# VectorE's order at the sub-layer ends of a two-layer trunk: chain, x update, split, low parts

## The chip, the cores and the metric

The kernel runs on one core of a Trainium2 chip. The metric is the time on the device of one execution, in microseconds (us). Before the change it is 2076.88 us, the median of three runs (2075.53 to 2077.28).

## The reference, cut to what matters

256 rows of 2048 numbers (fp32) go through two layers. A layer is a mixer and an MLP, each between two RMS norms and added to x:

```python
for layer in range(2):
    h = rms_norm(x, mix_pre_g[layer])
    m = pool_conformer_mixer(h, ...) if layer == 0 else short_conv_mixer(h, ...)
    x = x + rms_norm(m, mix_post_g[layer])
    h = rms_norm(x, ffn_pre_g[layer])
    a = relu(h @ w1[layer])                       # 2048 -> 8192
    x = x + rms_norm((a * a) @ w2[layer], ffn_post_g[layer])
# pool_conformer: h @ w_in (2048 -> 3072); pooling means over 2/4/8/16 rows, mixed by 4 groups;
#                 gated causal convolution of 31 taps, layer norm, silu; concatenation @ w_out
# short_conv:     h @ w_in (2048 -> 6144); B * conv3(C * u); @ w_out
```

So there are three places where one sub-layer ends and the next begins: end 1 (mixer of layer 0 to its MLP), end 2 (that MLP to the short convolution), end 3 (short convolution to the second MLP). At each, x must be updated with the norm over a whole row before the next matmul may read it.

## The kernel before

**Tiles.** The rows are two blocks of 128, t0 and t1. An output block is 128 rows by 512 columns in PSUM (pg), summed over k in steps of 128. Every fp32 product is three matmuls: with whi and wlo the high and low part of the weights, and xh and xl those of the transposed activations, whi x xh, wlo x xh and whi x xl (L224 to L226 in mms). A block with 8 k tiles has 24 matmuls, with 16 it has 48.

**Weights.** prep_to (L166) streams them in order, one tile of 128x1024 fp32 (512 KB, two k tiles) at a time: the SP queue loads raw (L170, four buffers), ScalarE rounds it to whi (L173), VectorE (in a front part GpSimd) subtracts to get wlo (L178). A raw buffer is free again once its wlo is made. whi and wlo have nine buffers each. ahead asks for the tiles of 4 or 8 steps ahead.

**An end.** The blocks of t0 are finished before those of t1, so that t1's last two blocks run on TensorE while t0's row is closed. At end 1 the last blocks are (0,0), (1,0), (0,1), (1,1) as (column block, row block). A block's result is first added to an earlier partial sum (L647 at end 1, L656 at end 2), then squared and summed on ScalarE (L591, L658) and multiplied with the gain (L592, L659). mix_close (L594) makes the square root on ScalarE (L601) and four tiny VectorE steps (L320 to L324). close_row (L343) updates x in four pieces of 512 columns (L355) and queues, per piece, norm_chunk: four transposes on TensorE (L276), xh on ScalarE in four pieces (L262), xl on VectorE in four pieces (L265). The next sub-layer's first block for t0 is mms_wide (L229): a first pass with whi over all k, xh and xl by turns (L240, L241), then a second pass with wlo (L248). Its low weight parts are so needed only in the second pass.

**What sets the order.** No order is written out. A scheduler places each instruction in its engine's queue by priority and the times it estimates; an engine then runs its queue strictly in that order, and an instruction that waits holds all behind it. urgent (L329) raises the priority by URGENT for the chain of an end. The low weight parts are ordinary work: wherever the scheduler sees VectorE free, one goes in.

**Other places that the change touches.** pool_sum (L448 on) multiplies PSUM sums with 1/count (L463) into an SBUF tile, which split_plain splits into ph and pl (L271, L272). The output projection's second half goes through its blocks as (2,0), (2,1), (3,0), (3,1), (0,0), (1,0), (0,1), (1,1) (L635); the layer norm of t0 and of t1 comes just before. The first sigmoid (L518) needs another function table on ScalarE than the square root before it.

## Time and profile before

| | |
|---|---|
| median of three runs | 2076.88 us |
| the profiled execution | 2074.67 us |
| its span | 2072.9 us |
| TensorE busy | 2041.4 us (98%) |
| VectorE busy | 1174.0 us (57%) |
| ScalarE busy | 1008.3 us (49%) |
| GpSimd busy | 153.5 us (7%), nearly all in the first 207 us |
| granted TensorE clock, mean | 0.995 |
| read from memory | 386.60 MB, 188 GB/s over the span |

In the rows PE is TensorE, PEld its weight load, DVE VectorE, ACT ScalarE, POOL GpSimd and SP the engine that issues the weight loads. A timeline row has the start, the duration (of all xN together), the engine, the line, what is written and read, the number of instructions and, in brackets, the idle time before it and what ended it. A row of waits has the waiting engine and line, the releaser, the sum in us, how many times, and the longest. In a row of windows each engine's busy time is followed by the number of its instructions. Matmuls overlap in the pipeline: one is recorded with 0.39 us, and the next starts 0.227 us after it. An engine that is busy half the time can still be full for ten microseconds at an end, so averages over the span say little here.

### The profile page before, as it was taken

What the parts mean: (1) busy time and instruction counts of PE and PEld (TensorE: products, weight loads), DVE (VectorE), ACT (ScalarE), POOL (GpSimd) and SP (SyncE); (2) the same over time, 40 slices, a digit from 0 to 9 for tenths busy, and PEclk for the clock granted to TensorE, in tenths of its full rate; (3) what the DMA queues carried; (4) which work ended last, traced back from release to release, by engine and by line L of the source; (5) the groups of instructions that cost most, each with busy time, mean ns of one, the idle gap of its engine ahead of it and who ended that gap; (6) DMA issues with size and microseconds to landing.
All of it is one profiled execution on the core that took longest, in us unless ns stands there. A gap on an engine that the chain in (4) does not pass through costs nothing.

```text
span 2072.9 us, 24556 instructions
## 1 busy us (share of the span) xinstructions
PE 2041.4 (98%) x9253; PEld 1687.7 (81%) x9253; DVE 1174.0 (57%) x1522; ACT 1008.3 (49%) x1296; POOL 153.5 (7%) x83
## 2 busy tenths in 40 slices
PE   8999999999999999999999999999999999999998
PEld 7888778888888888887888888888888888888886
DVE  3797764455455455547655645674555464554545
ACT  6454664444444354445544444464544444353443
POOL 5887000000000000000000000000000000000000
PEclk9999999999999999999999999999999999999999
DMA  7665546556565556556454665655555565565653
GB/s 261 198 208 180 176 148 219 175 180 210 171 203 181 184 194 198 186 170 213 161 197 165 201 197 177 202 189 193 183 193 193 170 212 187 171 208 189 201 172 114
DMA packets 203078, 390.30 MB, mean 188 GB/s; under 512 B 12368, under 2 KB 14512, under 8 KB 202960
## 3 DMA queue, kind: packets, MB, share of 16 engines
q1 hardware_dynamic: 202656, 388.55, 56.7%
q8 instruction: 72, 1.18, 0.2%
q14 instruction: 46, 0.38, 0.1%
q0 software_dynamic: 256, 0.18, 0.0%
q10 hardware_dynamic: 48, 0.02, 0.0%
HBM read 386.60 MB, written 2.10 MB: 188 GB/s over the span
## 4 chain that ended last, share of the span: by engine, by line
PE 85%; DVE 2%; DMA 1%; issue 1%; ACT 0%; DVEq 0%; ACTq 0%
PE pg L224 27%; PE pg L226 27%; PE pg L225 27%; PE pt L276 2%; DVE wlo L178 1%; DVE x L355 1%; PE pg L248 1%; PE pg L241 0%; DMA gp<-in_mix_post_g_dram 0%; PE pg L240 0%; DMA raw<-in_ab_w_out_dram 0%; ACT whi L173 0%; DVE xl L265 0%; DMA raw<-in_sc_w_in_dram 0%; DVE m L592 0%
## 5 line engine op out<-in xcount | busy, mean ns | idle before, releaser
L178 DVE TENSOR_TENSOR wlo<-raw,whi 128x1024 fp32r<-128x1024 f32 x660 | 807.5, 1227 | 580.4 <-ACT whi L173 547.9
L173 ACT CAST whi<-raw 128x1024 fp32r<-128x1024 f32 x722 | 760.2, 1054 | 575.2 <-PE pg L226 383.1
L226 PE MATMUL pg<-whi,xl 128*128 128x512 f32 x1520 | 596.0, 393 | 0.0
L224 PE MATMUL pg<-whi,xh 128*128 128x512 f32 x1520 | 590.9, 390 | 0.8 <-ACT t L518 0.7
L225 PE MATMUL pg<-wlo,xh 128*128 128x512 f32 x1520 | 591.3, 390 | 0.0
L225 PE MATMUL pg<-wlo,ah 128*128 128x512 f32 x1024 | 398.3, 389 | 0.0
L224 PE MATMUL pg<-whi,ah 128*128 128x512 f32 x1024 | 398.1, 389 | 0.0
L226 PE MATMUL pg<-whi,al 128*128 128x512 f32 x1024 | 397.6, 391 | 0.0
L225 PEld LDWEIGHTS pg<-wlo,xh 128*128 128x128 f32 x1520 | 285.4, 188 | 59.1
L224 PEld LDWEIGHTS pg<-whi,xh 128*128 128x128 f32 x1520 | 285.5, 188 | 58.5 <-ACT t L518 1.1
L226 PEld LDWEIGHTS pg<-whi,xl 128*128 128x128 f32 x1520 | 285.4, 188 | 56.9
L225 PEld LDWEIGHTS pg<-wlo,ah 128*128 128x128 f32 x1024 | 192.2, 188 | 40.1
L224 PEld LDWEIGHTS pg<-whi,ah 128*128 128x128 f32 x1024 | 192.3, 188 | 39.3
L226 PEld LDWEIGHTS pg<-whi,al 128*128 128x128 f32 x1024 | 192.3, 188 | 39.3
L178 POOL TENSOR_TENSOR wlo<-raw,whi 128x1024 fp32r<-128x1024 f32 x62 | 147.7, 2421 | 46.4 <-ACT whi L173 46.1
L680 ACT ACTIVATE t<-pg,rr 128x512 f32<-128x512 f32 x64 | 43.9, 686 | 194.0 <-PE pg L226 192.8
L711 DVE TENSOR_TENSOR m<-pg,m 128x512 f32<-128x512 f32 x96 | 65.9, 687 | 74.6 <-PE pg L226 74.6
L224 PE MATMUL pg<-whi,yh 128*128 128x512 f32 x256 | 100.2, 392 | 1.6 <-ACT yh L271 1.5
L225 PE MATMUL pg<-wlo,yh 128*128 128x512 f32 x256 | 99.7, 390 | 0.0
L226 PE MATMUL pg<-whi,yl 128*128 128x512 f32 x256 | 98.5, 390 | 0.2 <-DVE yl L272 0.2
L421 DVE SCALAR_TENSOR_TENSOR acc<-pp,par,acc 128x256 f32<-128x256 f32 x240 | 96.3, 480 | 0.1
L272 DVE TENSOR_TENSOR al<-pt,ah 128x512 fp32r<-128x512 f32 x64 | 44.0, 688 | 74.8 <-ACT ah L271 74.7
(130 smaller groups left out, 902.9 us busy)
## 6 DMA issues: line engine op xcount, KB each, us to landing
raw<-in_ffn_w_dram SPq DMA_DIRECT2D x512, 512.0 KB, 4.7
raw<-in_sc_w_in_dram SPq DMA_DIRECT2D x96, 512.0 KB, 4.9
raw<-in_ab_w_in_dram SPq DMA_DIRECT2D x48, 512.0 KB, 4.6
raw<-in_ab_w_out_dram SPq DMA_DIRECT2D x32, 512.0 KB, 3.9
raw<-in_sc_w_out_dram SPq DMA_DIRECT2D x32, 512.0 KB, 5.4
x<-in_x_dram SPq DMA_DIRECT2D x8, 256.0 KB, 7.2
gp<-in_mix_post_g_dram SPq DMA_DIRECT2D x8, 256.0 KB, 5.9
gp<-in_ffn_post_g_dram SPq DMA_DIRECT2D x8, 256.0 KB, 4.6
```

Source lines behind the costliest of these rows:

```text
L173: act.copy(hi, raw)
L178: (pool if on_pool else eng).tensor_tensor(lo[:, s], raw[:, s], hi.bitcast(F32)[:, s], ALU.subtract)
L224: pe.matmul(ps, lh, wh, start=start and k == 0, stop=False)
L225: pe.matmul(ps, lh, wl, start=False, stop=False)
L226: pe.matmul(ps, ll, wh, start=False, stop=stop and k == n - 1)
L248: pe.matmul(ps, lhs(k)[0], wt[c][1][:, j * CB : (j + 1) * CB], start=False, stop=k == n - 1)
L272: dve.tensor_tensor(lo, src, hi.bitcast(F32), ALU.subtract)
L276: pe.transpose(p[:, j * P : (j + 1) * P], src[:, j * P : (j + 1) * P], ident)
L355: dve.scalar_tensor_tensor(xs[t][:, cs], ms[t][:, cs], s, xs[t][:, cs], ALU.mult, ALU.add)
L421: dve.scalar_tensor_tensor(a, src, wcol, a, ALU.mult, ALU.add)
L680: act.activation(rl, ps, AF.Relu, scale=rr[t])
L711: dve.tensor_tensor(dst, ps, dst, ALU.add)
```

## The change

It gives VectorE another order at the three ends, by dependencies that bind the scheduler alone (hold, after): of the next sub-layer's weight tiles, the low parts of the second to fifth come after t0's second x update, those from the sixth on, and the first tile of the segment after, behind the last xl piece of t0's chunk 3, and the x update of t1's first 512 columns as well. The priority of urgent work goes from 150 to 1000. There are six raw buffers in place of four. The first two tiles of the segments after end 1 and end 2 have their hi and lo parts in the pool of the activations, not in that of the weights. In the output projection the partial sum is added in PSUM, with priority, and (3,0) comes before (2,1). In the pooling part the scaling stays in PSUM, its factors are loaded early in two pieces, and ph and pl are in another pool. A sigmoid of one column right after the row scales loads its table early.

```diff
+    RAW = 6
...
     def nm(s):
...
-    pool_lo = set()
-    for key in ("f1_0_0_0", "sC0", "f1_1_0_0"):
-        pool_lo |= set()
+    lows, guards = {}, {}
+    guests = set(seg["f1_0_0_0"][:2]) | set(seg["sC0"][:2])
+    def after(inst, first):
+        tc.add_manual_dep(
+            inst.ins, first.ins.name,
+            mybir.DependencyInfo(mybir.DependencyClass.NoSync, mybir.DependencyReason.SCHED_ONLY),
+            reason="row chain first")
+    def hold(ids, first):
+        for i in ids:
+            if i in lows:
+                after(lows[i], first)
+            else:
+                guards[i] = first
...
     def prep_to(i):
...
-            raw = wp.tile([P, 2 * CB], F32, tag="raw", name=nm("raw"), bufs=4)
+            raw = wp.tile([P, 2 * CB], F32, tag="raw", name=nm("raw"), bufs=RAW)
             nc.sync.dma_start(raw.rearrange("p (j n) -> p j n", j=nj), src)
-            hi = wp.tile([P, 2 * CB], F32R, tag="whi", name=nm("whi"))
-            lo = wp.tile([P, 2 * CB], F32R, tag="wlo", name=nm("wlo"))
+            home, tags = (ap_, ("ah", "al")) if nxt[0] in guests else (wp, ("whi", "wlo"))
+            hi = home.tile([P, 2 * CB], F32R, tag=tags[0], name=nm("whi"))
+            lo = home.tile([P, 2 * CB], F32R, tag=tags[1], name=nm("wlo"))
             act.copy(hi, raw)
-            i_, on_pool = nxt[0], nxt[0] in pool_lo
-            def low(raw=raw, hi=hi, lo=lo, on_pool=on_pool, eng=lo_eng[0](i_)):
-                for s in ((slice(0, CB), slice(CB, 2 * CB)) if on_pool else (slice(None),)):
-                    (pool if on_pool else eng).tensor_tensor(
-                        lo[:, s], raw[:, s], hi.bitcast(F32)[:, s], ALU.subtract)
-            low()
+            i_ = nxt[0]
+            low = lo_eng[0](i_).tensor_tensor(lo, raw, hi.bitcast(F32), ALU.subtract)
+            lows[i_] = low
+            if i_ in guards:
+                after(low, guards[i_])
...
-    URGENT = 150
+    URGENT = 1000
...
             pj = p[:, j * P : (j + 1) * P]
-            dve.scalar_tensor_tensor(
+            low = dve.scalar_tensor_tensor(
...
+        return low
...
         act.copy(hi, src)
...
     def norm_chunk(t, c, gkey, gbase):
...
-        split_cols(p, 4 * (c % 2), xT[t, c // 2], [pcol(gkey, gbase + 4 * c + j) for j in range(4)])
+        return split_cols(p, 4 * (c % 2), xT[t, c // 2],
+                          [pcol(gkey, gbase + 4 * c + j) for j in range(4)])
...
+    split_end = [None]
...
     def urgent(fn, *args):
         with tc.high_priority(URGENT):
-            fn(*args)
+            return fn(*args)
...
-    def close_row(t, s, nxt_gain, final=False):
+    def close_row(t, s, nxt_gain, final=False, nxt_ids=()):
...
-            dve.scalar_tensor_tensor(xs[t][:, cs], ms[t][:, cs], s, xs[t][:, cs], ALU.mult, ALU.add)
+            upd = dve.scalar_tensor_tensor(xs[t][:, cs], ms[t][:, cs], s, xs[t][:, cs],
+                                           ALU.mult, ALU.add)
+            if nxt_ids:
+                if t == 0 and c == 1:
+                    hold(nxt_ids[1:5], upd)
+                if t == NT - 1 and c == 0:
+                    after(upd, split_end[0])
...
-                later(2 + (c + 1) // 2, lambda c=c: urgent(norm_chunk, t, c, *nxt_gain))
+                def piece(c=c):
+                    end = urgent(norm_chunk, t, c, *nxt_gain)
+                    if t == 0 and c == 3:
+                        split_end[0] = end
+                        hold(nxt_ids[5:], end)
+                later(2 + (c + 1) // 2, piece)
...
         row_scale(t)
+    act.activation(small(), rr[NT - 1], AF.Sigmoid)
...
-            raw = wp.tile([P, 2 * CB], F32, tag="raw", name=nm("rw"), bufs=4)
+            raw = wp.tile([P, 2 * CB], F32, tag="raw", name=nm("rw"), bufs=RAW)
...
+        for h in range(2):
+            ic = mp.tile([P, 2 * T], F32, tag="gp", name=nm("ic"))
+            nc.sync.dma_start(ic, inv_cnt[2 * h * T : 2 * (h + 1) * T].partition_broadcast(P))
+            icnt[h] = ic
...
-        ic = t512((P, T))
-        nc.sync.dma_start(ic, inv_cnt[g * T : (g + 1) * T].partition_broadcast(P))
+        ic = icnt[g // 2][:, (g % 2) * T : (g % 2 + 1) * T]
...
-        pd = t512((P, 2, T))
-        dve.tensor_tensor(
-            pd, p.rearrange("p (c n) -> p c n", c=2),
-            ic.unsqueeze(1).to_broadcast([P, 2, T]), ALU.mult,
-        )
-        ph = tp.tile([P, 2, T], F32R, tag="ph", name=nm("ph"), bufs=2)
-        pl = tp.tile([P, 2, T], F32R, tag="pl", name=nm("pl"), bufs=2)
+        pd = p.rearrange("p (c n) -> p c n", c=2)
+        dve.tensor_tensor(pd, pd, ic.unsqueeze(1).to_broadcast([P, 2, T]), ALU.mult)
+        ph, pl = t512((P, 2, T), F32R), t512((P, 2, T), F32R)
         split_plain(pd, ph, pl)
...
-    def mix_close(t, parts, nxt_gain, final=False):
+    def mix_close(t, parts, nxt_gain, final=False, nxt_ids=()):
...
-        close_row(t, r, nxt_gain, final)
+        close_row(t, r, nxt_gain, final, nxt_ids)
...
-    for cb, t in ((2, 0), (2, 1), (3, 0), (3, 1), (0, 0), (1, 0), (0, 1), (1, 1)):
+    for cb, t in ((2, 0), (3, 0), (2, 1), (3, 1), (0, 0), (1, 0), (0, 1), (1, 1)):
...
-            dve.tensor_tensor(o, ps, o, ALU.add)
-            ps = o
+            urgent(dve.tensor_tensor, ps, ps, o, ALU.add)
         urgent(mix_evac, t, cb, ps, gps[cb], parts)
         if cb == 1:
-            urgent(mix_close, t, parts, ("ffn_pre", 0))
+            urgent(mix_close, t, parts, ("ffn_pre", 0), False,
+                   seg["f1_0_0_0"] + seg["f1_0_0_1"][:1])
     def last_evac(t, cb, ps, gp, parts):
...
                 if cb == NCB - 1:
-                    urgent(mix_close, t, parts, nxt_gain, final)
+                    urgent(mix_close, t, parts, nxt_gain, final,
+                           () if final else seg["sC0"] + seg["su0"][:1])
...
             if cb == NCB - 1:
-                urgent(mix_close, t, parts, ("ffn_pre", KT))
+                urgent(mix_close, t, parts, ("ffn_pre", KT), False,
+                       seg["f1_1_0_0"] + seg["f1_1_0_1"][:1])
```

What moves on VectorE (t0's x is x0, t1's is x1; wlo are low weight parts, sm the small columns of the norm's chain; the lines of the changed file are 14 to 30 higher: L178 is now L192, L265 L279, L355 L373, L656 L686). At end 2, from the chain's reciprocal to t0's x update, before:

```order
L320 RECIPROCAL sm_1482_7735<-sm_1481_7733 128x1
L178 TENSOR_TENSOR wlo_1471_7687<-raw_1469_7684,whi_1470_7686 128x1024
L322 TENSOR_SCALAR sm_1483_7737<-sm_1482_7735,sm_1480_7731 128x1
L178 TENSOR_TENSOR wlo_1474_7693<-raw_1472_7690,whi_1473_7692 128x1024
L323 TENSOR_SCALAR sm_1483_7737<-sm_1483_7737 128x1
L656 TENSOR_TENSOR pg_1488_7749<-pg_1488_7749,m_465_2530 128x512
L178 TENSOR_TENSOR wlo_1493_7794<-raw_1491_7791,whi_1492_7793 128x1024
L324 TENSOR_SCALAR sm_1482_7735<-sm_1482_7735,sm_1483_7737 128x1
L178 TENSOR_TENSOR wlo_1496_7800<-raw_1494_7797,whi_1495_7799 128x1024
L659 TENSOR_TENSOR m_465_2530<-pg_1488_7749,gp_1461_7666 128x512
L300 TENSOR_REDUCE sm_1509_7884<-parts_463_2528 128x1
L355 SCALAR_TENSOR_TENSOR x0_85<-m_464_2529,sm_1482_7735,x0_85 128x512 x4
```

and now, from the same place to the first xl:

```order
L630 TENSOR_SCALAR sm_1475_7725<-parts_457_2521,sm_1473_7721 128x1
L338 RECIPROCAL sm_1477_7729<-sm_1476_7727 128x1
L340 TENSOR_SCALAR sm_1478_7731<-sm_1477_7729,sm_1475_7725 128x1
L341 TENSOR_SCALAR sm_1478_7731<-sm_1478_7731 128x1
L342 TENSOR_SCALAR sm_1477_7729<-sm_1477_7729,sm_1478_7731 128x1
L373 SCALAR_TENSOR_TENSOR x0_85<-m_459_2523,sm_1477_7729,x0_85 128x512 x4
L192 TENSOR_TENSOR wlo_1463_7675<-raw_1461_7672,whi_1462_7674 128x1024
L192 TENSOR_TENSOR wlo_1466_7681<-raw_1464_7678,whi_1465_7680 128x1024
L192 TENSOR_TENSOR wlo_1469_7687<-raw_1467_7684,whi_1468_7686 128x1024
L192 TENSOR_TENSOR wlo_1488_7788<-raw_1486_7785,whi_1487_7787 128x1024
L686 TENSOR_TENSOR pg_1483_7743<-pg_1483_7743,m_460_2524 128x512
L279 SCALAR_TENSOR_TENSOR xl_1480_7736<-pt_1484_7768,par_96,xh_1479_7735 128x128 x4
```

Nothing stands between the chain's steps and the x update any more; four low parts and t1's add now follow it, and stand before the first xl.

At end 1, from the last step of the chain to the first xl, before:

```order
L324 TENSOR_SCALAR sm_426_2357<-sm_426_2357,sm_427_2359 128x1
L592 TENSOR_TENSOR m_361_2078<-opart_302_1810,gp_404_2263 128x512
L178 TENSOR_TENSOR wlo_440_2422<-raw_438_2419,whi_439_2421 128x1024
L300 TENSOR_REDUCE sm_453_2506<-parts_359_2076 128x1
L355 SCALAR_TENSOR_TENSOR x0_85<-m_360_2077,sm_426_2357,x0_85 128x512 x4
L178 TENSOR_TENSOR wlo_443_2428<-raw_441_2425,whi_442_2427 128x1024
L597 TENSOR_SCALAR sm_452_2505<-sm_453_2506 128x1
L647 TENSOR_TENSOR opart_302_1810<-pg_447_2437,opart_302_1810 128x512
L178 TENSOR_TENSOR wlo_446_2434<-raw_444_2431,whi_445_2433 128x1024
L178 TENSOR_TENSOR wlo_472_2538<-raw_470_2535,whi_471_2537 128x1024
L265 SCALAR_TENSOR_TENSOR xl_429_2364<-pt_433_2396,par_96,xh_428_2363 128x128 x4
```

and now:

```order
L342 TENSOR_SCALAR sm_421_2351<-sm_421_2351,sm_422_2353 128x1
L373 SCALAR_TENSOR_TENSOR x0_85<-m_355_2071,sm_421_2351,x0_85 128x512 x4
L192 TENSOR_TENSOR wlo_408_2299<-raw_406_2296,whi_407_2298 128x1024
L192 TENSOR_TENSOR wlo_411_2305<-raw_409_2302,whi_410_2304 128x1024
L192 TENSOR_TENSOR wlo_414_2311<-raw_412_2308,whi_413_2310 128x1024
L350 TENSOR_TENSOR pg_427_2365<-pg_427_2365,opart_297_1804 128x512
L192 TENSOR_TENSOR wlo_432_2410<-raw_430_2407,whi_431_2409 128x1024
L350 TENSOR_TENSOR pg_442_2431<-pg_442_2431,opart_297_1804 128x512
L279 SCALAR_TENSOR_TENSOR xl_424_2358<-pt_428_2390,par_96,xh_423_2357 128x128 x4
```

T1's product, a low part and a reduction no longer stand before the update; three low parts, t1's first add, one more low part and t1's second add do before xl. Some rows further on, at the last xl pieces of t0's chunk 3, it now reads:

```order
L279 SCALAR_TENSOR_TENSOR xl_426_2360<-pt_445_2482,par_96,xh_425_2359 128x128 x2
L373 SCALAR_TENSOR_TENSOR x1_86<-m_356_2072,sm_451_2507,x1_86 128x512 x2
L279 SCALAR_TENSOR_TENSOR xl_426_2360<-pt_445_2482,par_96,xh_425_2359 128x128
L373 SCALAR_TENSOR_TENSOR x1_86<-m_356_2072,sm_451_2507,x1_86 128x512
L279 SCALAR_TENSOR_TENSOR xl_426_2360<-pt_445_2482,par_96,xh_425_2359 128x128
L373 SCALAR_TENSOR_TENSOR x1_86<-m_356_2072,sm_451_2507,x1_86 128x512
```

The dependency holds only the update of t1's first column piece, the last row here; the other three stand between the pieces of chunk 3's xl. Before, all four stood ahead of chunk 2's and chunk 3's xl.

In the pooling part (acc is the convolution's sum, t in the first excerpt a scaled sum in SBUF, pt a sum in PSUM), before:

```order
L463 TENSOR_TENSOR t_268_1597<-pt_267_1588,t_266_1586 128x512
L421 SCALAR_TENSOR_TENSOR acc_206_1122<-pp_422,par_96,acc_206_1122 128x256
L421 SCALAR_TENSOR_TENSOR acc_207_1123<-pp_422,par_96,acc_207_1123 128x256
L421 SCALAR_TENSOR_TENSOR acc_206_1122<-pp_422,par_96,acc_206_1122 128x256
L272 TENSOR_TENSOR pl_270_1600<-t_268_1597,ph_269_1599 128x512
L421 SCALAR_TENSOR_TENSOR acc_207_1123<-pp_422,par_96,acc_207_1123 128x256
L421 SCALAR_TENSOR_TENSOR acc_206_1122<-pp_422,par_96,acc_206_1122 128x256
L463 TENSOR_TENSOR t_274_1634<-pt_273_1625,t_272_1623 128x512
L421 SCALAR_TENSOR_TENSOR acc_207_1123<-pp_422,par_96,acc_207_1123 128x256
L421 SCALAR_TENSOR_TENSOR acc_206_1122<-pp_422,par_96,acc_206_1122 128x256
L421 SCALAR_TENSOR_TENSOR acc_207_1123<-pp_422,par_96,acc_207_1123 128x256
L272 TENSOR_TENSOR pl_276_1637<-t_274_1634,ph_275_1636 128x512
```

and now:

```order
L497 TENSOR_TENSOR pt_265_1586<-pt_265_1586,ic_194_1076 128x512
L452 SCALAR_TENSOR_TENSOR acc_209_1128<-pp_424,par_96,acc_209_1128 128x256
L452 SCALAR_TENSOR_TENSOR acc_210_1129<-pp_424,par_96,acc_210_1129 128x256
L497 TENSOR_TENSOR pt_269_1620<-pt_269_1620,ic_194_1076 128x512
L452 SCALAR_TENSOR_TENSOR acc_209_1128<-pp_424,par_96,acc_209_1128 128x256
L287 TENSOR_TENSOR t_267_1597<-pt_265_1586,t_266_1596 128x512
L452 SCALAR_TENSOR_TENSOR acc_210_1129<-pp_424,par_96,acc_210_1129 128x256
L452 SCALAR_TENSOR_TENSOR acc_209_1128<-pp_424,par_96,acc_209_1128 128x256
L287 TENSOR_TENSOR t_271_1631<-pt_269_1620,t_270_1630 128x512
```

The two scalings come closer together, and the subtraction (L287, L272 before) reads pt in PSUM where it read t in SBUF; five convolution steps instead of eight stand between the first scaling and the last subtraction.

## The prediction

> **What bounds the kernel now.** I read the first row of the page, then TensorE's waits, then the windows in which it is not full. The first row and the waits:
>
> ```profile
> PE 2041.4 (98%) x9253; PEld 1687.7 (81%) x9253; DVE 1174.0 (57%) x1522; ACT 1008.3 (49%) x1296; POOL 153.5 (7%) x83
> ...
> PE pg L241 <- DVE xl L265: 5.8, 4, 2.7
> PE pt L101 <- DMA t<-in_mix_pre_g_dram: 4.6, 1, 4.6
> PE pg L240 <- ACT xh L262: 4.0, 2, 2.2
> PE pt L492 <- DVE pl L272: 2.5, 1, 2.5
> PE pg L224 <- ACT yh L271: 1.5, 1, 1.5
> ...
> PE pg L224 <- ACT t L518: 0.7, 1, 0.7
> PE pg L226 <- DVE yl L272: 0.2, 1, 0.2
> ```
>
> TensorE is busy 2041.4 of the 2072.9 us span, so 31.5 us is all that any reordering can win, apart from time at a lower clock. 4.6 us is the first DMA, and the tail after the last matmul takes about ten more; the diff leaves both alone. What it can touch is xl and xh (9.8 us, the starts of the next sub-layer), pl and yh (4.0 us, the pooling and the layer norm) and t (0.7 us). The windows say where (columns: us, PE busy, weight loads, DVE, ACT, POOL, granted clock, DMA share, GB/s):
>
> ```profile
> 164.00:170.00 6.00, 3.53 (x22) 3.01 (x21) 6.00 (x11) 3.47 (x5) 6.00 (x3) 1.00 0.67 224
> ...
> 220.00:225.00 5.00, 3.84 (x17) 2.66 (x15) 3.42 (x9) 4.83 (x8) 0.00 (x0) 1.00 0.11 43
> ...
> 255.00:260.00 5.00, 3.24 (x17) 2.10 (x15) 5.00 (x8) 3.17 (x6) 0.00 (x0) 0.98 0.90 271
> 260.00:265.00 5.00, 2.03 (x4) 1.33 (x5) 5.00 (x12) 4.97 (x17) 0.00 (x0) 0.50 0.81 246
> 265.00:270.00 5.00, 4.90 (x22) 3.58 (x21) 4.86 (x14) 2.82 (x11) 0.00 (x0) 0.84 0.61 215
> 270.00:275.00 5.00, 4.85 (x25) 4.05 (x26) 3.96 (x18) 3.54 (x13) 0.00 (x0) 1.00 0.00 0
> 975.00:980.00 5.00, 4.56 (x22) 3.47 (x20) 4.73 (x10) 2.88 (x5) 0.00 (x0) 1.00 0.89 321
> 980.00:985.00 5.00, 1.74 (x9) 0.98 (x9) 5.00 (x8) 4.37 (x12) 0.11 (x1) 0.84 0.71 209
> 985.00:990.00 5.00, 3.79 (x11) 3.12 (x12) 4.86 (x16) 2.62 (x9) 0.00 (x0) 0.50 0.87 305
> ...
> 1350.00:1355.00 5.00, 4.11 (x20) 3.15 (x19) 5.00 (x15) 4.65 (x14) 0.00 (x0) 1.00 0.91 284
> ```
>
> End 1 (mixer to FFN 0) is idle 1.76+2.97+0.10+0.15 = 5.0 us, and end 2 (FFN 0 to short conv) 0.44+3.26+1.21 = 4.9. VectorE is full in both, and the granted clock falls to 0.50. What that costs is at most busy time times missing clock, 0.50x2.03+0.16x4.90 = 1.8 us at end 1 and 0.16x1.74+0.50x3.79 = 2.2 at end 2; I take three quarters, 1.3 and 1.6, since recorded matmul times overlap. So the ends cost 6.3 and 6.5. End 3 (short conv to FFN 1) is idle 0.89 at full clock.
>
> Why VectorE is late at end 2, from the timelines of DVE, ACT and PE; the last three rows are the same chain at end 3:
>
> ```profile
> 968.71 0.70 DVE L656 TENSOR_TENSOR pg<-pg,m 128x512 f32<-128x512 f32 x1 [2.52 <-PE pg L226]
> 971.02 0.29 ACT L601 ACTIVATE sm<-parts,sm 128x1 f32<-128x1 f32 x1
> 972.30 0.16 DVE L320 RECIPROCAL sm<-sm 128x1 f32<-128x1 f32 x1
> 972.51 1.22 DVE L178 TENSOR_TENSOR wlo<-raw,whi 128x1024 fp32r<-128x1024 f32 x1
> 979.09 2.73 DVE L355 SCALAR_TENSOR_TENSOR x<-m,sm,x 128x512 f32<-128x512 f32 x4
> 985.80 1.38 DVE L265 SCALAR_TENSOR_TENSOR xl<-pt,par,xh 128x128 fp32r<-128x128 f32 x5
> ...
> 978.93 0.39 PE L225 MATMUL pg<-wlo,ah 128*128 128x512 f32 x1
> 979.16 0.39 PE L226 MATMUL pg<-whi,al 128*128 128x512 f32 x1
> 983.04 0.51 PE L240 MATMUL pg<-whi,xh 128*128 128x512 f32 x1 [1.76 <-ACT xh L262]
> 986.21 0.80 PE L241 MATMUL pg<-whi,xl 128*128 128x512 f32 x1 [2.66 <-DVE xl L265]
> ...
> 1337.22 0.15 DVE L320 RECIPROCAL sm<-sm 128x1 f32<-128x1 f32 x1
> 1338.15 1.23 DVE L178 TENSOR_TENSOR wlo<-raw,whi 128x1024 fp32r<-128x1024 f32 x1
> 1339.30 2.74 DVE L355 SCALAR_TENSOR_TENSOR x<-m,sm,x 128x512 f32<-128x512 f32 x4
> ```
>
> t0's last block ends at T0 = 968.6. The square root is there at 971.3, yet the x update starts at 979.09: five low parts of 1.22 us, t1's add and its product stand before and between the four tiny steps of the chain, which alone take 0.93 (end 3, 1337.22 to 1338.15). Matmuls start 0.227 us apart, so t1's two blocks (48) cover only up to T0+10.9, where transposes need an x that is just ready; three more low parts then stand before xl.
>
> **The change part by part.** All sums are against the profiled execution.
>
> *Ends: x update first.* At end 2 the root comes at 971.02 as now, since add, square and one cast stay ahead of it. After its 0.29 the reciprocal follows at once or, at the latest, where it is today, 972.30; then 0.93 of small steps with nothing between. So the x update starts between T0+3.7 and T0+4.6; I take T0+4.3, and it ends at T0+7.05, before t1's blocks do. The transposes then wait for nothing. What is late next is xl: behind the update stand four held low parts (4 x 1.2) and one add (0.7), and a piece of xl takes 1.38/5 = 0.28, so the first is done at T0+12.9. TensorE is through t1's blocks and the transposes at about T0+11.8 and waits 1.1. Later in the same pass chunk 2's xh stands on ACT behind three casts and two squares (0.15 wait), and chunk 3's xl pieces alternate on VectorE with t1's x updates (2.73/4 = 0.68 each): a piece every 0.96 where a pair of matmuls takes 0.45, so waits of about 1.0, 0.95 and 0.5. Together 3.7 in small pieces. None is near the 4.9 us over which the clock fell, so I take no half clock: 6.5-3.7 = **2.8 gained**, bounds 0.5 (a first gap that still halves the clock) and 5.
>
> *End 1*, from its own rows:
>
> ```profile
> 248.56 0.69 DVE L592 TENSOR_TENSOR m<-opart,gp 128x512 f32<-128x512 f32 x1 [1.78 <-DMA gp<-in_mix_post_g_dram]
> 256.65 2.73 DVE L355 SCALAR_TENSOR_TENSOR x<-m,sm,x 128x512 f32<-128x512 f32 x4
> 263.36 0.86 DVE L265 SCALAR_TENSOR_TENSOR xl<-pt,par,xh 128x128 fp32r<-128x128 f32 x3
> ```
>
> Here T0 is 246.1. A second cast (1.0) stands before the root, so the update runs from T0+5.2 to T0+8.0 (before: T0+10.6 to T0+13.3). The gain vector's DMA, which kept m to T0+2.5, is still under the root's time. Behind the update come four low parts and both of t1's adds (4.8+1.3): xl at about T0+14.4, TensorE free at T0+11.7, wait 2.7; then chunk 3's pieces between t1's updates again, 2.15. Of 6.3 remain 4.85: **1.5 gained**. If 2.7 us of idleness halves the clock, nothing is gained; if t1's second add is not late, 2.5.
>
> In the rows above the clock had fallen after 4.9 us of idleness in two pieces with one matmul between, and had not after 0.89. [...]
>
> *End 3* has one low part ahead of its update today (1338.15) and no idle window before chunk 2. Moving that part behind the update brings x 1.1 earlier, for nothing. But three of t1's four updates (2.05) now stand before chunk 3's xl: **1.1 lost**, bounds 0 and 2.
>
> *Pooling.* The sums are scaled in PSUM, so the subtraction for pl reads PSUM and one SBUF tile instead of two SBUF tiles:
>
> ```profile
> 159.88 0.67 DVE L463 TENSOR_TENSOR t<-pt,t 128x512 f32<-128x512 f32 x1
> 161.65 1.64 DVE L272 TENSOR_TENSOR pl<-t,ph 128x512 fp32r<-128x512 f32 x1
> 163.21 0.87 DVE L421 SCALAR_TENSOR_TENSOR acc<-pp,par,acc 128x256 f32<-128x256 f32 x2
> 165.77 2.66 DVE L272 TENSOR_TENSOR pl<-t,ph 128x512 fp32r<-128x512 f32 x1
> ```
>
> GpSimd is busy all through this stretch (the window from 164). The same size took 0.67 with a PSUM operand and 1.64 and 2.66 without. The order from 159.88 is now two scalings, two subtractions and five convolution steps (0.43): 4 x 0.65 + 5 x 0.4 = 4.6, so the last pl is done near 164.5. Today it is done at 168.4, at the end of TensorE's wait of 2.5, so that wait goes: **2.5 gained**. Were the subtractions as slow as now, it would be done 3.0 later, at 167.5, and 1.0 gained. [...]
>
> *Output projection.* (3,0) now runs before (2,1): 24 matmuls, 5.4 us, between the layer norm of t0 and the first use of t1's yh. That covers the 1.5 and the 0.2 of the waits: **1.7 gained**, bounds 0.5 and 1.7.
>
> *Sigmoid table* loaded ahead: **0.7 gained**, bounds 0 and 0.7.
>
> *Six raw buffers and the gains' early load.* In the long stages TensorE is already full, so deeper loading buys nothing there. At the start two weight tiles (1 MB) go ahead of the last x chunks. The rate in the first 40 us, one slice per us:
>
> ```profile
> GB/s 0 37 131 142 352 363 404 396 380 315 352 393 387 381 385 387 391 387 381 389 385 289 2 133 352 119 227 348 350 229 289 88 174 301 131 307 182 207 231 195
> ```
>
> At 390 those chunks come 2.7 us later; the squares on them stand on ACT before xh of chunk 2. I take **0.4 lost**, bounds 0 and 1.5. The two guest tiles and the in-place adds change no instruction's length.
>
> Sum: -2.8 - 1.5 + 1.1 - 2.5 - 1.7 - 0.7 + 0.4 = -7.7, so 2074.67 - 7.7 = 2067.0. The median of the runs shown is 2.2 above the profiled execution: **2069.2 us**.
>
> **Rivals.** *The waits are replaced.* VectorE does the same work in the same stretch; xl is as late as x was. For it: the held low parts and adds before xl, t1's updates before chunk 3. Against it: the update is 6 us earlier and only 5 stand behind it. Ends 1 and 2 then give 0, end 3 loses 2, and 4.9-0.4 remain from the rest: 2074.4.
>
> *Slower.* ACT takes its instructions in order, and casts that wait for a held-back raw stand before its squares, root and xh at all three ends. A raw is freed only by a low part, and those are held until the update; the next load then needs a landing time:
>
> ```profile
> raw<-in_sc_w_in_dram SPq DMA_DIRECT2D x13, 512.0 KB, 4.8
> ```
>
> That is the median. At T0+8.3 plus 4.8 the cast is just in time for xh of chunk 2 at T0+17. With 7 or 8 us it is 3 late at each end, and with the half clock 1.5 more: 4.5 a time, 13.5 in all against my -7.7: 2082.7. From 1.2 us per end it takes the change back to within 0.2%, from 2.6 the kernel is slower than before. Against it: six buffers load two tiles more before the end begins.
>
> *Full gain.* The ends' remaining 3.7 and 4.85 shrink by half, 4.3 less: 2064.9; with end 3 unharmed 2063.8. For it: each wait there is a piece or two of other work ahead of xl. Against it: that work stands in VectorE's queue as shown, whatever the times are.
>
> **Chances.** Forecast and its near neighbours 0.55, waits replaced 0.23, slower 0.12, full gain 0.10. A change within 0.2% (4.2 us) cannot be told from none. Faster by more means below 2072.7: the forecast case and the full gain, 0.65. Same: the replaced waits and a tenth of the slower case, 0.24. Slower: the rest, 0.11. Terms' bounds give 2062.5 to 2072.5 for the likeliest case; the range takes in the replaced waits: 2061.5 to 2077.5.
>
> **What would show it.** x update of t0 starting within 6 us of T0 at ends 1 and 2; no wait of the transposes for x; first xl waits of 2.7 and 1.1; clock 1.00 in the windows around them; no wait of TensorE for pl, yh or the sigmoid; a larger wait than 0.9 at end 3. I am wrong if the clock still halves, if ACT waits for raws ahead of xh, or if a wait turns up in the long stages.

## The result, and the profile after

The changed kernel takes 2060.02 us (median, 2059.55 to 2060.63), the kernel before 2076.89 (2075.53 to 2077.28): a ratio of 0.992, 95% interval 0.9903 to 0.9937, or 16.9 us less. The forecast was 2069.2, 7.7 less; the measured time lies below its range of 2061.5 to 2077.5.

The page's first row and TensorE's waits of the kernel after:

```profile
PE 2037.4 (99%) x9253; PEld 1685.5 (82%) x9253; DVE 1169.9 (57%) x1522; ACT 1006.9 (49%) x1297; POOL 153.7 (7%) x83
...
PE pt L102 <- DMA t<-in_mix_pre_g_dram: 4.6, 1, 4.6
PE pg L255 <- DVE xl L279: 3.7, 6, 1.4
PE pt L291 <- DMA x<-in_x_dram: 1.6, 2, 1.4
PE pg L254 <- ACT xh L276: 0.2, 1, 0.2
```

The waits for pl, yh and the sigmoid's t are gone, those for xl and xh have shrunk from 9.8 us to 3.9. TensorE is also busy 4.0 us less with the same 9253 matmuls, because none of them runs at half clock between the start and the tail (before, 6.83 us passed at half clock at each of ends 1 and 2). The windows, with the same columns as before:

```profile
220.00:225.00 5.00, 5.00 (x24) 4.12 (x23) 3.43 (x5) 4.85 (x8) 0.00 (x0) 1.00 0.00 0
...
250.00:255.00 5.00, 3.63 (x21) 2.76 (x20) 5.00 (x11) 3.77 (x12) 0.00 (x0) 1.00 0.93 306
255.00:260.00 5.00, 4.94 (x26) 3.78 (x25) 3.80 (x14) 5.00 (x13) 0.00 (x0) 1.00 0.64 218
260.00:265.00 5.00, 4.11 (x16) 2.47 (x15) 4.81 (x12) 3.02 (x11) 0.00 (x0) 1.00 0.00 0
...
975.00:980.00 5.00, 4.11 (x18) 2.60 (x16) 4.02 (x14) 5.00 (x17) 0.00 (x0) 1.00 0.31 107
980.00:985.00 5.00, 4.16 (x20) 2.89 (x19) 5.00 (x8) 1.13 (x4) 0.10 (x1) 1.00 0.11 9
...
1340.00:1345.00 5.00, 4.98 (x26) 4.03 (x26) 5.00 (x9) 0.38 (x3) 0.00 (x0) 1.00 0.22 48
```

End 1 is idle 1.37+0.06+0.89 = 2.3 us (before 5.0), end 2 0.89+0.84 = 1.7 (4.9), end 3 0.02 (0.9), all at full clock. VectorE's timeline shows the chain as it was meant, with the add of t0's last block, the x update and the first xl of ends 1 and 2:

```profile
240.58 0.70 DVE L350 TENSOR_TENSOR pg<-pg,opart 128x512 f32<-128x512 f32 x1 [2.98 <-PE pg L240]
...
245.12 2.74 DVE L373 SCALAR_TENSOR_TENSOR x<-m,sm,x 128x512 f32<-128x512 f32 x4
...
253.51 2.15 DVE L279 SCALAR_TENSOR_TENSOR xl<-pt,par,xh 128x128 fp32r<-128x128 f32 x8
...
959.22 0.70 DVE L686 TENSOR_TENSOR pg<-pg,m 128x512 f32<-128x512 f32 x1 [2.98 <-PE pg L240]
...
962.81 2.74 DVE L373 SCALAR_TENSOR_TENSOR x<-m,sm,x 128x512 f32<-128x512 f32 x4
...
970.61 1.11 DVE L279 SCALAR_TENSOR_TENSOR xl<-pt,par,xh 128x128 fp32r<-128x128 f32 x4
```

Both traces hold the same number of matmuls, so the start of the matmul that follows the first n tells where the time went. The differences are worked out from the two lists; where the order of two blocks differs they are good to about 0.4 us.

| up to | n | before, us | after, us | after - before | this stage | forecast |
|---|---|---|---|---|---|---|
| the first blocks | 100 | 28.3 | 28.9 | +0.6 | +0.6 | +0.4 |
| the first sigmoid | 250 | 62.5 | 62.2 | -0.4 | -1.0 | -0.7 |
| the pooling | 750 | 170.2 | 167.5 | -2.7 | -2.3 | -2.5 |
| the layer norm | 1025 | 226.8 | 221.3 | -5.5 | -2.8 | -1.7 |
| end 1 | 1400 | 314.8 | 305.3 | -9.5 | -4.0 | -1.5 |
| end 2 | 4525 | 1014.4 | 1000.4 | -14.0 | -4.5 | -2.8 |
| end 3 | 6100 | 1363.2 | 1348.1 | -15.2 | -1.1 | +1.1 |

So 15 us is what the profiled executions differ by (2074.67 and 2059.65). The other 1.9 of the 16.9 come from the kernel before: its profiled execution was 2.2 below its median, that of the change 0.4.

### The profile page after: what moved, and what is told of

Same layout as the page of the kernel before. It is cut to its first block, busy times and chain, and to the rows that moved or that the text cites. A ratio compares the mean times of both kernels' runs of the same rounds, so it can differ in the third digit from the quotient of the medians.

```text
span 2057.9 us, 24531 instructions
## 1 busy us (share of the span) xinstructions
PE 2037.4 (99%) x9253; PEld 1685.5 (82%) x9253; DVE 1169.9 (57%) x1522; ACT 1006.9 (49%) x1297; POOL 153.7 (7%) x83
## 4 chain that ended last, share of the span: by engine, by line
PE 98%; ACT 1%; DMA 1%; DVE 1%; SPq 0%; issue 0%; DVEq 0%; ACTq 0%
PE pg L239 31%; PE pg L240 31%; PE pg L238 31%; PE pt L291 2%; PE pg L262 1%; PE pg L404 0%; PE pg L405 0%; DMA x<-in_x_dram 0%; PE pg L403 0%; ACT whi L190 0%; ACT xh L276 0%; DVE x L373 0%; PE pg L255 0%; DMA raw<-in_sc_w_in_dram 0%; PE pt L522 0%; PE pt L493 0%
## 5 line engine op out<-in xcount | busy, mean ns | idle before, releaser
L192 DVE TENSOR_TENSOR wlo<-raw,whi 128x1024 fp32r<-128x1024 f32 x660 | 803.6, 1224 | 493.1 <-ACT whi L190 452.5
L192 POOL TENSOR_TENSOR wlo<-raw,whi 128x1024 fp32r<-128x1024 f32 x62 | 147.9, 2423 | 44.7 <-ACT whi L190 44.6
L286 ACT CAST ah<-pt 128x512 fp32r<-128x512 f32 x64 | 37.4, 584 | 135.2 <-PE pt L291 135.2
L287 DVE TENSOR_TENSOR al<-pt,ah 128x512 fp32r<-128x512 f32 x64 | 44.0, 687 | 96.5 <-ACT ah L286 96.4
```

The costliest lines, as they stand in the source:

```text
L192: low = lo_eng[0](i_).tensor_tensor(lo, raw, hi.bitcast(F32), ALU.subtract)
L286: act.copy(hi, src)
L287: dve.tensor_tensor(lo, src, hi.bitcast(F32), ALU.subtract)
```

## The experiments

Theory A: VectorE's held order carries the ends. Theory B: the buffers do, the six raws and the guest tiles. In each diff - stands for the kernel that it starts from. Those marked as one execution have one time and one profile beside the median of the kernel before; they are read by their traces.

**Without the dependencies.**

```diff
 # from the change
-                if t == 0 and c == 1:
-                    hold(nxt_ids[1:5], upd)
-                if t == NT - 1 and c == 0:
-                    after(upd, split_end[0])
+                pass
...
-                        hold(nxt_ids[5:], end)
```

> The change without its scheduling dependencies (no low part and no x update is held); all else stays. Theory A: the held order makes the gain at the three ends (4.0 + 4.4 + 1.1 = 9.5 us of the 15 by which the span fell). Then the x update of t0 starts late again, the clock halves again after ends 1 and 2, and the time is 2060.0 + 9.5 = 2069.5, between 2067 and 2071. Theory B: the six raw buffers, the guest tiles and the in-place adds carry the ends; then the time stays at or below 2062 and the clock stays full.

Measured: 2071.57 us (2071.17 to 2072.31), ratio to the kernel before 0.9974 (0.9964 to 0.9983). Against the trace of the change, end 1 costs 5.4 us more, end 2 5.0, end 3 1.8. TensorE's timeline, and one window:

```profile
254.78 1.97 PE L291 MATMUL pt<-ident,x 128*128 128x128 f32 x8 [3.77 <-DVE x L373]
258.94 0.79 PE L255 MATMUL pg<-whi,xl 128*128 128x512 f32 x1 [1.77 <-DVE xl L279]
...
981.36 0.79 PE L255 MATMUL pg<-whi,xl 128*128 128x512 f32 x1 [4.45 <-DVE xl L279]
...
255.00:260.00 5.00, 3.23 (x12) 2.53 (x12) 5.00 (x13) 4.07 (x16) 0.00 (x0) 0.50 0.88 306
```

The waits for x and xl are back, and the half clock with them. Without the dependencies the rest of the change makes the ends worse than they were. Theory A holds, with 11.5 in place of 9.5, which is a little above its range.

**The dependencies alone.** The functions hold and after, with their calls, in the kernel before; no other line of the change.

> The kernel before with the scheduling dependencies alone: four raw buffers, no guest tiles, the old priority, partial sums added in SBUF, old pooling, block order and sigmoid. Theory A: the ends gain nearly all of their 9.5 us, 2076.9 - 9.5 = 2067.4, between 2066 and 2069.5. Theory B: with four raw buffers the held low parts keep the raws, casts on ScalarE wait for loads ahead of xh and the ends gain less than half: 2072 or more.

Measured: 2066.11 us (2065.29 to 2067.48), ratio 0.9949 (0.9934 to 0.9963), 11.6 below the kernel before on that chip. By the trace ends 1 and 2 are as good as in the change (end 1 0.6 better), end 3 is not (1.4 worse). TensorE's waits:

```profile
PE pg L258 <- DVE xl L282: 3.4, 7, 0.7
PE pt L524 <- DVE pl L290: 2.5, 1, 2.5
PE pg L241 <- ACT yh L289: 1.5, 1, 1.5
```

Theory A holds. What is left to the whole change, 6.1 us by the times, is by the trace (8.1, its execution being the slowest of the four) 0.6 at the first sigmoid, 2.6 at the pooling, 4.1 at the layer norm and 1.4 at end 3.

**Four raw buffers.** One execution.

```diff
 # from the change
-    RAW = 6
+    RAW = 4
```

> The change with four raw buffers in place of six; VectorE's order at the ends is the same. Theory A: no effect beyond the start, where six cost about half a microsecond: 2059 to 2061. Theory B: the casts come late at the ends: 2063 or more, with waits of ScalarE for raws ahead of xh.

Measured: 2066.17 us, 6.1 more. Theory A was wrong here: the chains of the ends stand in the same order, but TensorE loses 5.1 us at the layer norm, 0.5 at end 2 and 1.3 at end 3. VectorE's timeline at the layer norm in this run and in the change, from the low part ahead of t0's steps to the reciprocal of t1's, with one wait of TensorE behind it in the run:

```profile
195.17 3.28 DVE L192 TENSOR_TENSOR wlo<-raw,whi 128x1024 fp32r<-128x1024 f32 x1 [4.32 <-ACT whi L190]
198.37 0.28 DVE L592 TENSOR_SCALAR t<-pt 128x128 f32<-128x128 f32 x1
...
210.24 0.95 DVE L596 RECIPROCAL t<-t 128x128 f32<-128x128 f32 x1
...
222.97 0.50 PE L238 MATMUL pg<-whi,yh 128*128 128x512 f32 x1 [2.10 <-ACT yh L286]
```

```profile
194.62 1.96 DVE L192 TENSOR_TENSOR wlo<-raw,whi 128x1024 fp32r<-128x1024 f32 x1 [4.91 <-ACT whi L190]
196.51 0.28 DVE L592 TENSOR_SCALAR t<-pt 128x128 f32<-128x128 f32 x1
...
207.97 0.95 DVE L596 RECIPROCAL t<-t 128x128 f32<-128x128 f32 x1 [0.31 <-ACT t L594]
```

The low part starts 0.5 later and takes 1.3 longer, so t0's steps start 1.9 later. In both runs GpSimd makes its own beside it (190.28 to 197.36 here, 190.78 to 198.8 in the change); the next one in the change, at 205.84 with GpSimd idle, took 1.23. With fewer buffers the scheduler also puts more casts and low parts between the steps, and t1's reciprocal is 2.3 later. TensorE waits 2.1 us for yh, with (3,0) before (2,1): the new block order does not cover that. ScalarE hardly waits for loads here (1.9 us from 185 to 240). So the buffers act through the order and a slow low part; which of the two weighs more was read from rows, not tried apart. At end 3 the load itself is late, on ScalarE ahead of the Square that VectorE's chain needs:

```profile
1339.30 1.05 ACT L190 CAST whi<-raw 128x1024 fp32r<-128x1024 f32 x1 [1.00 <-DMA raw<-in_ffn_w_dram]
```

**The old block order.** One execution.

```diff
 # from the change
-    for cb, t in ((2, 0), (3, 0), (2, 1), (3, 1), (0, 0), (1, 0), (0, 1), (1, 1)):
+    for cb, t in ((2, 0), (2, 1), (3, 0), (3, 1), (0, 0), (1, 0), (0, 1), (1, 1)):
```

> The change with the old block order of the output projection, (2,1) before (3,0). Theory A: the block between covers t1's yh, so TensorE waits for it again: 1.5 to 2.2 us more than the change, 2061.5 to 2062.5, with the wait behind the layer norm. Theory B: since with four raw buffers the wait for yh was there in spite of the new order (2.1 us), the six buffers are what removes it: 2060 within 0.7 and no such wait.

Measured: 2059.48 us, and by the trace no difference anywhere above 0.2 us. With six raw buffers the swap is worth nothing, which is theory B.

**Six raw buffers alone.** One execution. Six raw buffers do not fit beside the rest as it is (the pool of the work tiles needs 22 KB per partition, and 15.4 are left), so ph and pl share the buffers of the other 512-column tiles.

```diff
 # from the kernel before
-            raw = wp.tile([P, 2 * CB], F32, tag="raw", name=nm("raw"), bufs=4)
+            raw = wp.tile([P, 2 * CB], F32, tag="raw", name=nm("raw"), bufs=6)
...
-        ph = tp.tile([P, 2, T], F32R, tag="ph", name=nm("ph"), bufs=2)
-        pl = tp.tile([P, 2, T], F32R, tag="pl", name=nm("pl"), bufs=2)
+        ph, pl = t512((P, 2, T), F32R), t512((P, 2, T), F32R)
```

> The kernel before with six raw buffers and, for the space, ph and pl in the pool of the other 512-column tiles; nothing else. Theory A: the buffers alone take away the wait for yh behind the layer norm and the one at end 3, while VectorE's order at ends 1 and 2 leaves those as they were: 2.5 to 3.5 below the kernel before. Theory B, that of the prediction: the buffers gain nothing by themselves, within 0.8 of it.

Measured: 2074.13 us. That is 1.2 below the lowest of the six executions of the kernel before that ran beside it (2075.37 to 2078.81), but an execution of the kernel before on another chip took 2074.07; the span is only 0.5 below that of before. Its waits of TensorE:

```profile
PE pg L241 <- DVE xl L265: 9.6, 5, 4.4
...
PE pg L224 <- DVE m L591: 1.7, 1, 1.7
```

The wait for t1's yh has turned into one for m: a PSUM buffer of a finished block, which VectorE empties only behind the layer norm's steps. At ends 1 and 2 xl is waited for longer than before, 4.4 us each, and xh no longer. Neither theory fits well. The time says 2.8 less, the trace 0.5: by themselves the buffers move waits and gain little.

**Dependencies and six raw buffers.** One execution: the edits of the dependencies alone and of the six buffers alone, together on the kernel before.

> The kernel before with the scheduling dependencies and six raw buffers, ph and pl as in the run before; no guest tiles, old block order, old pooling arithmetic, no early sigmoid table. Theory A: these two parts carry the change: against it 2.5 to 3.5 for pooling and the table are missing and 3.6 for the guests are won, 2060 - 0.6, between 2058 and 2061.5. Theory B: the parts overlap, so that the buffers add less than 3 to the dependencies alone (2066.1): 2063 or more.

Measured: 2059.26 us, the time of the whole change. The two together gain 17.6 us, the dependencies alone 11.6: the buffers add 6.0 here, 6.8 by the two times themselves, against 0.5 to 2.8 alone. Theory A holds. Against the trace of the dependencies alone, 8.2 us longer, it gains 1.1 up to the first sigmoid, 1.8 at the pooling and the layer norm, 2.0 at end 1, 1.9 at end 2 and 1.5 at end 3.

**The pooling operand.** One execution.

```diff
 # from the change
-        pd = p.rearrange("p (c n) -> p c n", c=2)
-        dve.tensor_tensor(pd, pd, ic.unsqueeze(1).to_broadcast([P, 2, T]), ALU.mult)
+        pd = t512((P, 2, T))
+        dve.tensor_tensor(pd, p.rearrange("p (c n) -> p c n", c=2), ic.unsqueeze(1).to_broadcast([P, 2, T]), ALU.mult)
```

> The change with the scaled pooling sums written to an SBUF tile again, so that the subtraction for pl reads two SBUF operands beside GpSimd; all else stays. Theory A: pl takes 1.6 to 2.7 us instead of 0.7 and TensorE waits for it 0.5 to 2.5: 2060.5 to 2062.5. Theory B: the closer order of the scalings is the gain, pl is in time even when slow: 2060 within 0.7, no wait.

Measured: 2060.22 us. VectorE's timeline of the last two subtractions, and TensorE's wait for them; then the same two in the change:

```profile
159.76 2.62 DVE L287 TENSOR_TENSOR t<-t,t 128x512 fp32r<-128x512 f32 x1
164.08 1.12 DVE L287 TENSOR_TENSOR t<-t,t 128x512 fp32r<-128x512 f32 x1
...
PE pt L522 <- DVE t L287: 0.2, 1, 0.2
```

```profile
160.89 0.68 DVE L287 TENSOR_TENSOR t<-pt,t 128x512 fp32r<-128x512 f32 x1
162.27 0.68 DVE L287 TENSOR_TENSOR t<-pt,t 128x512 fp32r<-128x512 f32 x1
```

With two SBUF operands the subtraction is slow again beside GpSimd (busy from 152.83 to 171.76 in the change), 2.62 and 1.12 us in place of 0.68. The one for yl, of the same size and with two SBUF operands as well, takes 0.69 at 206.93 in this run, by when GpSimd has long finished in the change (198.8). The slow ones cost 0.2 of a wait, no more: the last pl is done at 165.2, and TensorE needs it at about 165. The gain at the pooling is from when these instructions run, not from their operand.

**The sigmoid's table.** One execution.

```diff
 # from the change
-    act.activation(small(), rr[NT - 1], AF.Sigmoid)
```

> The change without the early load of the sigmoid's table. Theory A: TensorE waits for the first sigmoid again, 0.7 to 1.0 more: 2060.7 to 2061. Theory B: other work covers it now, no such wait, 2060 within 0.5.

Measured: 2060.28 us; TensorE does not wait for the sigmoid, and until end 2 begins the trace shows no difference above 0.2 us. At end 2 this execution loses 0.7: two casts wait 0.39 and 0.69 us for their loads there, ahead of chunk 2's xh, and the clock falls to half (see the last section). The 1.0 that the change gains at the first sigmoid comes with six raw buffers as well: alone they have it too (the 250th matmul 1.2 us earlier relative to the 25th), and the row of that wait is missing from their list. With six buffers the early table load (1.28 us on ScalarE in the change) does nothing. With four raw buffers and the early load the wait is gone too, so there the load may do it; that was not tried apart.

**All of t1's updates held.** One execution, for the small waits left at the ends.

```diff
 # from the change
-                if t == NT - 1 and c == 0:
+                if t == NT - 1:
                     after(upd, split_end[0])
```

> The change with all four of t1's x updates held behind the last xl piece of t0, not the first alone. Theory A: the waits of 0.65 and 0.19 between those pieces at ends 1 and 2 go, 2060.0 - 1.7 = 2058.3, between 2057.5 and 2059. Theory B: they only move to t1's transposes, 2060 within 0.7.

Measured: 2059.44 us. The last pieces of xl are no longer waited for, but now low parts are. TensorE's waits:

```profile
PE pg L255 <- DVE xl L279: 2.0, 2, 1.4
...
PE pg L239 <- DVE wlo L192: 1.2, 3, 0.4
```

At ends 1 and 2 the trace gets 1.4 us ahead of the change for a moment and keeps 0.4 and 0.5 of it; end 3 gives 0.8 back. Theory B has the time right, but the waits moved to the low parts and not to t1's transposes: VectorE has then four updates (2.7 us) between the splits and the low parts of the second pass.

**Without guest tiles.** One execution first, then four.

```diff
 # from the change
-    guests = set(seg["f1_0_0_0"][:2]) | set(seg["sC0"][:2])
+    guests = set()
```

> The change without the guest tiles: the first two tiles of the segments after ends 1 and 2 have their hi and lo in the weight pool again. Without them t1's x updates come later in VectorE's order at ends 1 and 2. Theory A: the guests carry nothing, 2058.5 to 2061. Theory B: without them the whi of the last tiles come late, 2063 or more.

Measured: 2055.71 us. Both theories had it wrong: it is faster.

> The change without the guest tiles, timed in rounds. Theory A: the 4 us of the one look hold, 2055.5 to 2057, 1.0% below the kernel before, since low parts come before t1's updates and the first xl before t1's add. Theory B: they were chance, 2059 to 2060.5.

Measured: 2055.26 us (2054.31 to 2055.95), ratio 0.9895 (0.9877 to 0.9913). End 1 of that run, on VectorE:

```profile
251.80 1.12 DVE L279 SCALAR_TENSOR_TENSOR xl<-pt,par,xh 128x128 fp32r<-128x128 f32 x4
252.84 0.69 DVE L350 TENSOR_TENSOR pg<-pg,opart 128x512 f32<-128x512 f32 x1
...
258.91 3.48 DVE L192 TENSOR_TENSOR wlo<-raw,whi 128x1024 fp32r<-128x1024 f32 x3
...
263.63 2.73 DVE L373 SCALAR_TENSOR_TENSOR x<-m,sm,x 128x512 f32<-128x512 f32 x4
```

With no other edit the scheduler places t1's second add behind the first four xl pieces, and four low parts before t1's x updates. TensorE waits for no xl. That the guests cost the change nearly 5 us is shown; that they do it through this order is how the rows read, and was not tried apart.

**Three parts alone.** The dependencies, the six raw buffers and the pooling part on the kernel before: the change less guest tiles, block order, in-place and urgent adds, sigmoid, and with the old priority.

> Three parts of the change alone on the kernel before: the scheduling dependencies, six raw buffers, and the pooling part (scaling in PSUM, factors loaded early). Old block order, partial sums added in SBUF, old priority, no guest tiles, no early sigmoid table. Theory A: these three are all that pays; the wait for m behind the layer norm (1.7 with two of them) is gone, since the pooling part puts that m earlier into VectorE's order; the time is that of the change without guests, 2055.3, plus up to 0.7 for the table: 2055 to 2056.3. Theory B: the block order or the in-place adds are needed for the layer norm or end 1: 2057 or more.

Measured: 2055.08 us (2054.80 to 2055.93), ratio 0.9898 (0.9881 to 0.9914), 21.3 below the kernel before on that chip. All of TensorE's waits, and the m that TensorE waited 1.7 us for with the dependencies and six buffers alone:

```profile
PE pt L102 <- DMA t<-in_mix_pre_g_dram: 4.5, 1, 4.5
PE pt L291 <- DMA x<-in_x_dram: 1.1, 1, 1.1
PE pt L291 <- DVE x L373: 0.9, 2, 0.5
...
216.79 0.68 DVE L621 TENSOR_TENSOR m<-pg,gp 128x512 f32<-128x512 f32 x1
```

Theory A holds: three parts are all that pays. They beat the kernel before by 21 us and the whole change by 4 to 5. The in-place adds and the priority were left out only here, together with the rest, and not tried apart.

## Why the prediction was wrong

The direction, the places and most mechanisms were right; the size was not, and two causes were put down to the wrong part. By the prediction's own steps:

**What bounds the kernel.** Right. All gains are gaps of TensorE at the places named and the half clock behind them, and the long stages did not move.

**End 2 (2.8 forecast, 4.5 measured).** The price of the end, 6.5, was about right: 4.5 gained and 1.7 left make 6.2. The chain ran as worked out; with T0 = 959.1 the update starts at T0+3.7, the early end of the interval. The mis-sized term is the waits that stay, 3.7 forecast and 1.7 measured. The update came 0.6 before the T0+4.3 that was taken, and four low parts and an add took 5.1 us with their overlap (965.47 to 970.61) where 4 x 1.2 + 0.7 = 5.5 was taken, so the first piece of xl was done at T0+11.8 and not T0+12.9. TensorE is there at T0+11.9: a wait of 1.1 was forecast, none came.

```profile
971.02 0.48 PE L255 MATMUL pg<-whi,xl 128*128 128x512 f32 x1
```

Chunk 2 cost 0.17 for xh, as forecast, and 0.67 for its xl, which the sum did not have. Chunk 3's pieces, forecast at 2.45, cost 0.65 and 0.19. I had an update of t1 ahead of each piece, but two pieces are done before the first update stands in their way.

**End 1 (1.5 forecast, 4.0 measured).** The price of 6.3 was right (4.0 gained, 2.3 left), and again the update came earlier and the work behind it took less than was taken. With T0 = 240.5 the update started at T0+4.6 (5.2 forecast), and the first piece of xl was done at T0+13.3 (14.4). TensorE's waits in the change:

```profile
253.91 0.50 PE L255 MATMUL pg<-whi,xl 128*128 128x512 f32 x1 [1.36 <-DVE xl L279]
262.86 0.49 PE L255 MATMUL pg<-whi,xl 128*128 128x512 f32 x1 [0.65 <-DVE xl L279]
263.78 0.50 PE L255 MATMUL pg<-whi,xl 128*128 128x512 f32 x1 [0.19 <-DVE xl L279]
```

1.36 where 2.7 was forecast, 0.84 where 2.15 was: 2.2 in place of 4.85.

**The clock.** It stayed full, as the sum had it, but the premise was wrong and the step held by the smaller waits. I took the clock to have fallen over 4.9 us of idleness. In the trace of the kernel before it falls at 983.4, after waits of 0.44 and 1.76 and before the one of 2.66 begins. No run shows that the 2.7 us forecast for end 1 would leave the clock full: the longest wait after the first loads that did is 2.47 (pl in the kernel before), and behind 2.10 with four raw buffers and 2.46 with the dependencies alone it was halved.

**End 3 (1.1 lost forecast, 1.1 gained measured).** The step "three of t1's four updates now stand before chunk 3's xl" describes the order rightly, and the updates are where it says. They hold nothing up, since xl of chunk 2 now comes before t1's updates and not behind low parts. The term had the wrong sign. The gain needs the six buffers: with four of them TensorE waits 0.7 for xl and the stage is 1.3 longer.

**Six raw buffers.** This is the step that failed in kind. "Deeper loading buys nothing there" was argued from the long stages. It looked at the rate of loading alone, and not at what the buffers let the scheduler put where. With four the change is 6.1 us slower, mostly by a later chain at the layer norm. The mechanism of the slower rival, a cast that waits for its raw ahead of xh, is real but small. With four buffers it shows at end 2 (0.89, and TensorE then waits 0.71 for xh), and at end 3 a cast waits 1.00 ahead of a Square. With six it shows at end 2 (0.51, and TensorE waits 0.17). The dependencies without the two more buffers stop at 2066.

**Output projection (1.7 forecast for the swap).** The gain came, 2.8, and the swap has no part in it: undone, nothing changes, and with four buffers it does not cover the wait. Six buffers remove the wait for yh and, alone, leave one of 1.7 for m. With the pooling part it is gone too; by the rows the scheduler then puts that m in the middle of the layer norm's steps.

**Pooling (2.5 forecast, 2.3 measured).** The size was right. The faster subtraction is real (0.68 with a PSUM operand, 1.12 and 2.62 with two SBUF operands beside GpSimd) and buys 0.2. With slow subtractions 2.1 are still gained, where the step put 1.0. In that run the scalings are no closer together than before. The first starts 1.9 us earlier (157.98, before 159.88), six convolution steps in place of eight stand behind it, and the last subtraction takes 1.12 in place of 2.66. Which of these weighs most was not tried apart.

**Sigmoid's table (0.7).** The wait went, but with six buffers it goes without the early load.

**Guest tiles and in-place adds.** "Change no instruction's length" is true (an add takes 0.70 us in PSUM and took 0.69, a low part 1.22 and 1.23 on average) and beside the point: they change what the scheduler makes of the rest, and the guests cost nearly 5 us.

**Chances and range.** Faster had 0.65 and came true. The full-gain case (2063.8, chance 0.10) was nearest, and its halved waits were about right: 4.0 us are left at ends 1 and 2 of the 8.55 forecast. The argument against it, that the work ahead of xl stands in the queue "whatever the times are", overlooked that work in a queue costs only where TensorE arrives before it is done. The time lies below even this case by three steps: 1.1 gained at end 3, 1.1 more at the layer norm, and the 2.2 that were added from the profiled execution to the median, which in the changed kernel are 0.4. With 2.2 the time would have been 2061.9, just inside the range, and by luck, since the mechanisms above would have been as wrong.

## What to carry to other kernels

Where one engine runs an ordered queue, move the chain that releases the next stage ahead of the work that may come later, and see whether there are buffers enough for what is put off: here the order alone gave 11.6 us, the buffers alone 0.5 to 2.8, both together 17.6. Undo the parts of a bundled change one at a time, since with an automatic scheduler a part that looks neutral can cost: block order, in-place adds, priority and the sigmoid's table together did nothing, and the guest tiles took back nearly 5 us. When a wait is forecast from a queue, work out both when the work is done and when the waiting engine arrives.

## What the runs showed of the hardware

Behind waits of about 2 us TensorE's clock was halved in two runs. In the run with four raw buffers the wait for yh (2.10, quoted above) is followed by 3.41 us at half clock. In the run with the dependencies alone, the wait of 2.46 for pl (166.22 to 168.68) has half clock behind it as well:

```profile
166.50:169.90 3.40, 1.22 (x7) 1.13 (x8) 3.40 (x5) 1.91 (x4) 3.40 (x2) 1.00 0.57 195
169.90:173.30 3.40, 3.40 (x12) 2.83 (x12) 3.40 (x9) 0.04 (x1) 3.31 (x2) 0.50 0.69 216
```

In the kernel before, the wait for pl is as long (2.47, 166.01 to 168.48), and the clock stays full:

```profile
164.20:167.60 3.40, 1.81 (x12) 1.47 (x10) 3.40 (x5) 2.74 (x4) 3.40 (x2) 1.00 0.67 219
167.60:171.00 3.40, 2.52 (x14) 2.21 (x15) 3.40 (x8) 0.73 (x2) 3.40 (x3) 1.00 0.66 230
```

Two short waits had it behind them too. In the run without the early sigmoid TensorE waits 0.88 and 0.66 us at end 2, and 3.41 us at half clock follow:

```profile
974.40:977.80 3.40, 1.86 (x10) 1.11 (x9) 1.43 (x5) 3.32 (x8) 0.00 (x0) 1.00 0.36 98
977.80:981.20 3.40, 3.40 (x9) 2.62 (x9) 3.17 (x11) 3.40 (x13) 0.00 (x0) 0.50 0.21 77
```

A single wait of 1.71 with six buffers alone, the same with the dependencies and six buffers (mean granted clock of the run 0.999), and one of 1.36 in the change left the clock full. The stretches at one clock, 249.17, 6.83, 716.80, 6.83 and 1075.20 us in the kernel before, are all whole multiples of 3.413 us (73, 2, 210, 2 and 315), and the windows shown are laid on that grid. In the run with the dependencies alone 2.2 of the 2.46 us of waiting fall into one window, in the kernel before the 2.47 us are split into 1.6 and 0.9. So waits of the same length had different outcomes; that their place on the grid decides is my estimate from these two runs and was not tried. Idleness in a window is not all that counts, since behind 1.54 the clock was halved and behind 1.71 it was not; the former's window also holds four transposes. What else counts was not tried, nor whether this is part of why the kernel before varies by 3 us and the changed one by 1.
